# An encoder layer's grid attention: sets of equal length, scores seven steps ahead, and the last input projection ended half by half

## The chip, the cores and the metric

One Trainium2 chip, of which the kernel uses one core. The metric is the device time of one execution in microseconds, lower is better; the time of a kernel is the median of its runs. Engines: PE (TensorE, the matmuls), DVE (VectorE), ACT (ScalarE), POOL (GpSimd) and SP (SyncE, which here only issues DMAs). PEld is the weight load of PE.

## What is computed

One encoder layer on 1024 tokens of width 1024, all in float32:

```
hn   = rmsnorm(h);  proj = hn @ w_in            # 1024 x 2304 columns
o_a  = window attention, 8 heads of 64, 2 kv heads, |i-j| <= 128, a sink logit per head
o_b  = neighbourhood attention, 8 heads of 64, on the 16 x 64 grid of tokens,
       window 8 x 16, with a bias by 2-D offset
h    = h + concat(rmsnorm(o_a), rmsnorm(o_b)) @ w_out
h    = h + (silu(conv3(hn2 @ w_gate)) * (hn2 @ w_up)) @ w_down
out  = rmsnorm(h)
```

## The kernel before

**Precision.** Each float32 operand is held as a high and a low part in the type of the fast matmul. A product of two such operands is three matmuls of 128x512 (`block`, lines 176 to 179): high by high, high by low, low by high. The low part costs a subtraction on DVE, the high part a copy on ACT.

**Stages.** First the input projection: 18 column tiles of 128 (`Project`, m = 0 to 17). Tiles 0 to 5 feed the window heads. From m = 6 on each pair of grid heads has three tiles: the values of both heads, then query and key of the one and of the other, so that head 6 of the grid needs m = 16 and head 7 needs m = 17. Then follow attention, the out projection (`OutA`, the window half, lines 600 to 626; the grid half after it) and the gated MLP, which takes the time from about 365 us to the end.

**How attention and projections are mixed.** PE runs in the order in which the Python code issues (PE alone has a manual schedule). On the other engines the tile framework's scheduler orders the instructions, with priorities. Lines 887 to 914 write PE's order: `flat` holds 16 window units and then 32 grid units, four per grid head. A grid head has eight blocks of 128 queries (`q_step`) and eight blocks of 128 keys (`t_step`), and the four units hold 1, 2, 2 and 3 of the latter (`chunks`, line 556). In each unit there are three kinds of events:

- "q": scores of one query block (line 389, two matmuls into one of two PSUM banks "s"), then its softmax (lines 412 to 420): bias and row minimum on DVE, the exponential on ACT, and for each pair of blocks the scaling on POOL;
- "t", called a set in what follows: two or three transposes of 128x128 (line 526, name pt), whose result is split into ph (ACT, line 426) and pl (DVE, line 427);
- "v": the value products of the set before (lines 537 and 538, which need ph and pl). A set's value products come one set later, behind the next set's transposes.

After each event `fill` draws blocks of three matmuls from `filler`, a generator that runs the rest of the projections and then `OutA`: `RATES` says how many per window of eight units or per grid head, and a unit of a grid head gets a quarter of its head's number, whatever its sets. Scores are drawn with `q_until(u + 2)`: all those of the next two units, at the places 1, 3, 5 and so on of the unit's events. Where scores need a projection that isn't done, `run_q` draws filler blocks until it is; these aren't counted in `debt`.

**From projection to scores.** When a projection's two halves have gone through PSUM (two banks "pj"), `evacuate` scales them on DVE (line 251 for the grid). After some more filler blocks `post` calls `split_qk` (lines 301 to 313): for each half a high part on ACT (line 306) and a low part on DVE (line 307), and then four DMAs on SP's queue that stack parts on the upper and lower partitions: q from a's upper half (line 309), q from b's upper half (310), b's upper half from a's lower one (311), and a's upper half from b's lower one (312). Line 311 overwrites what line 310 reads, and line 312 what line 309 reads. Only then can the head's first scores run.

**The last projection.** m = 17 (lines 582 to 593) runs its two halves in turns, k by k, so that both end together, and between the k steps it makes the high and low parts of the normed window output (`split`, lines 187 to 191: one 128x1024 copy on ACT and one 128x1024 subtraction on DVE, four times), which take over the buffers of the projection's input. Both halves are evacuated at the end; the first `OutA` block takes the bank of the first half.

Of the kernel before, what the change touches and what calls it, by code (L numbers as in the profile page):

```python
# [14 lines left out]
F32R = mybir.dt.float32r  # L15
AF = mybir.ActivationFunctionType
ALU = mybir.AluOpType
# [3 lines left out]
KT = D // 128  # L21
# [12 lines left out]
RATES = [41, 50, 21, 21, 21, 21, 13, 19, 20, 17]  # L34
SPARE = (3, 6)
AHEAD = 2
EVA = (1, 3, 5, 8)
WARM = 8

# [17 lines left out]
def hybrid_layer(tc, xT, w_first, w_in, w_out, w_gate, w_up, w_down, small, sink, rpb, consts, rope, out):  # L57
    nc = tc.nc
    with ExitStack() as ctx:
# [13 lines left out]
        def big(name, tag, dt=F32):  # L73
            return lpool.tile([128, S], dt, name=name, tag=tag, bufs=slots[tag])

        def tmp(name, dt=F32, n=S):
            return tpool.tile([128, n], dt, name=name, tag="t", padded_shape=[128, S + 16])

        def bank(name, tag):
            return psum.tile([128, HALF], F32, name=name, tag=tag)  # L80

        f32 = lambda ap: ap.bitcast(F32)
        tsl = lambda h: slice(h * HALF, (h + 1) * HALF)
# [16 lines left out]
        flat = lambda t, n: t[:, 0:n * 384].rearrange("p (k c) -> p k c", c=384)  # L100
# [3 lines left out]
        for name, dst, n in (("h", his, 2), ("h", his, 2), ("l", los, 2), ("l", los, 2), ("w", None, 2)):  # L104
            t = flat(big(name, "mix", F32R)[:, :], n)
# [46 lines left out]
        def behind(*names):  # L152

            stack = ExitStack()
            for n in names:
                stack.enter_context(tc.issue_after(mark[n].ins))
            return stack
# [18 lines left out]
        def block(ps, w, x, h, first, last):  # L176
            nc.tensor.matmul(ps, w[0], mv(x[0][:, tsl(h)]), start=first, stop=False)  # L177
            nc.tensor.matmul(ps, w[0], mv(x[1][:, tsl(h)]), start=False, stop=False)  # L178
            nc.tensor.matmul(ps, w[1], mv(x[0][:, tsl(h)]), start=False, stop=last)  # L179

        def product(ps, ws, xs, h):

            for i, (w, x) in enumerate(zip(ws, xs, strict=True)):
                block(ps, w, x, h, i == 0, i == len(ws) - 1)
                yield

        def split(src, name, tag):
            hi, lo = big(name + "h", tag, F32R), big(name + "l", tag, F32R)
            nc.scalar.activation(hi, src, AF.Copy)
            nc.vector.tensor_tensor(lo, src, f32(hi[:, :]), op=ALU.subtract)  # L190
            return hi, lo

        def squares(tiles, engine):
            acc = None
# [49 lines left out]
        def evacuate(t, ps, h, grid):  # L244
            if not grid:
                mark["copied"] = nc.vector.tensor_tensor(sv(t[:, tsl(h)]), pv(ps[:, :]), sv(rstd1[:, tsl(h)]), op=ALU.mult)
            else:
                o = t[:, :].rearrange("p (b r s c) -> p r s b c", r=ROWS // 2, s=2, c=8)[:, 4 * h:4 * h + 4]
                i = ps[:, :].rearrange("p (r b c s) -> p r s b c", s=2, b=NB, c=8)
                v = rstd1[:, tsl(h)].rearrange("p (r s b c) -> p r s b c", s=2, b=NB, c=8)  # L250
                nc.vector.tensor_tensor(o, i, v, op=ALU.mult)
# [99 lines left out]
        mix = [None] * 8  # L351
# [14 lines left out]
        def post(m, t):  # L366

            if m < 6:
                turn(m, t)
                stacks(m, t)  # L370
            else:
                hp, i = divmod(m - 6, 3)
                if i == 0:
                    vb[2 * hp], vb[2 * hp + 1] = split_v(t, (0, 1), lambda: done.add(m))
                else:
                    h = 2 * hp + i - 1
                    qb[h], kb[h] = split_qk(t)
# [183 lines left out]
        mg, h1, norm = [None] * 8, [None] * KT, {"halves": 0}  # L561

        class Project:
# [10 lines left out]
            def run(self):  # L574
                self.t = tmp("t")
                if self.m < 17:
                    for h in range(2):
                        ps = bank("pj", "pj")
                        yield from product(ps, self.w, xg, h)
                        with tc.high_priority(offset=500), behind(*["low"] * (self.m == 3 and h == 1)):  # L580
                            evacuate(self.t, ps, h, self.grid)
                else:

                    ps = [bank("pj", "pj") for _ in range(2)]
                    for k in range(KT):
                        for h in range(2):
                            block(ps[h], self.w[k], xg[k], h, k == 0, k == KT - 1)
                            yield
                        if k % 2:
                            mg[k // 2] = split(mix[k // 2], "mg", "xg")  # L590
                    with tc.high_priority(offset=500):
                        for h in range(2):
                            evacuate(self.t, ps[h], h, self.grid)

            def post(self):
                post(self.m, self.t)
                if self.m < 6 or self.m % 3:
                    done.add(self.m)

        class OutA:  # L600
            def __init__(self, d):
# [27 lines left out]
        xg, first = [None] * KT, [Project(m) for m in range(3)]  # L629
# [58 lines left out]
        t = quarters(big("f", "mix"))  # L688
# [136 lines left out]
        def fill(n):  # L825
            while n > 0 and next(filler, False):
                n -= 1
# [3 lines left out]
        for g in range(2):  # L831
            for b in range(NB):
                q, t = unit_window(g, b)
# [7 lines left out]
        flat = []  # L841
        for u, (q, t, need, kind, ahead) in enumerate(units):
            flat.append((q, t, need, kind))
        debt = 0.0
# [6 lines left out]
        order = []  # L851
# [3 lines left out]
        def q_until(u, limit):  # L855
            nonlocal qpos
            res = []
            while qpos < len(queue_q) and queue_q[qpos][0] <= u and len(res) < limit:
                res.append(queue_q[qpos])
                qpos += 1  # L860
            return res

        def run_q(items):
            for u, s in items:
                while any(m not in done for m in flat[u][2]):
                    assert next(filler)
                s()

        sums = {}

        def square_b(u):

            if u == 40:
                sums["b"] = big("sqb", "op")
                for h in range(2):
                    nc.scalar.activation(sums["b"][:, tsl(h)], mix[4][:, tsl(h)], AF.Square)
            s2 = tmp("sq")
            for h in range(2):
                nc.scalar.activation(s2[:, tsl(h)], mix[5 if u == 40 else 6][:, tsl(h)], AF.Square)
                nc.vector.tensor_tensor(sums["b"][:, tsl(h)], sums["b"][:, tsl(h)], s2[:, tsl(h)], op=ALU.add)  # L880

        pend = None
        for i, item in enumerate(q_until(1, 4 + AHEAD)):
            run_q([item])
            fill(i % 2 + 1)
        fill(FILL1 - 9)
        for u in range(len(flat)):
            q, t, need, kind = flat[u]
            if kind == 0 and u < 14:
                mine = q_until(u + 2, 4)  # L890
            else:
                mine = q_until(min(u + 2, len(flat) - 1), 99)
            events = []
            for ts in t:
                events += [("t", ts), ("v", None)]
            for i, item in enumerate(mine):
                events.insert(min(EVA[i] if kind == 0 else 2 * i + 1, len(events)), ("q", item))
            wi = u // 8 if u < 16 else 2 + (u - 16) // 4
            per = RATES[wi] / (8 if u < 16 else 4) / len(events)
            if u in (40, 44):  # L900
                square_b(u)
            for what, e in events:
                if what == "t":
                    nxt = e()
                elif what == "v":
                    if pend is not None:
                        pend()
                    pend = nxt
                else:
                    run_q([e])  # L910
                debt += per
                fill(int(debt))
                debt -= int(debt)
            live["op"] -= 7 if u in (7, 15) else 4 if u >= 16 and u % 4 == 3 else 0
        with tc.high_priority(offset=500), behind("high"):
            nc.scalar.activation(warm, eps, AF.Sqrt)
# [23 lines left out]
        for h in range(2):  # L940
            wide = widen(vb2[h], "pt")
            for i in range(4):
                x = mix[4 + i][:, tsl(h)]
                hi, lo = (t[:, tsl(h)] for t in mg[4 + i])
# [111 lines left out]
        for h in range(2):  # L1056
            for d in range(KT):
                if h == 0 and d + 2 < KT:
                    wo.append(load_wo(d + 2, False))
                ps = bank("pj", ("o", "s", "pj")[(h * KT + d) % 3])  # L1060
# [4 lines left out]
                if h == 1 and d == 1:  # L1065
                    v = inverse_narrow([total[0]], D, "pt")
# [148 lines left out]
        v = inverse_narrow([total[1]], D, "pt")  # L1215
# [50 lines left out]
        order = []  # L1266
# [71 lines left out]
        for i, f in enumerate(FO[HEAD:]):  # L1338
            u = Gated(f)
# [117 lines left out]
        for i, (p, j, c) in enumerate(order):  # L1457
# [10 lines left out]
            ps = banks[p, j]  # L1468
# [8 lines left out]
            q = i % 12  # L1477
# [16 lines left out]
        parts = {}  # L1494
        for k, cols in enumerate(quarters):
            for j in (2, 3):
                ps = banks[6, j]
# [111 lines left out]
```

## Time and profile before

| | us |
|---|---|
| median of 3 runs | 1029.18 (1029.17 to 1029.4) |
| the profiled execution's own time | 1030.14 |
| its span, first to last instruction | 1028.4 |
| PE busy in the span | 1011.9 (98%) |
| DVE, ACT, POOL busy | 836.6, 560.6, 107.7 |

Busy time on PE is rough: matmuls overlap, and a matmul's end is modelled, so that a short stop can hide inside the one before it. Where it matters the distance between the starts of two matmuls is the better measure. The rows of a timeline give start, duration, engine, line, operation, output and inputs; in brackets stands the idle time before the row and what ended it. A queue's name with q at the end (SPq) is the issue of a DMA, not its transfer.

### The profile page before, as it was taken

What the parts mean: (1) busy time and instruction counts of PE and PEld (TensorE: products, weight loads), DVE (VectorE), ACT (ScalarE), POOL (GpSimd) and SP (SyncE); (2) the same over time, 40 slices, a digit from 0 to 9 for tenths busy, and PEclk for the clock granted to TensorE, in tenths of its full rate; (3) what the DMA queues carried; (4) which work ended last, traced back from release to release, by engine and by line L of the source; (5) the groups of instructions that cost most, each with busy time, mean ns of one, the idle gap of its engine ahead of it and who ended that gap; (6) DMA issues with size and microseconds to landing.
All of it is one profiled execution on the core that took longest, in us unless ns stands there. A gap on an engine that the chain in (4) does not pass through costs nothing.

```text
span 1028.4 us, 14846 instructions
## 1 busy us (share of the span) xinstructions
PE 1011.9 (98%) x5094; PEld 889.3 (86%) x5094; DVE 836.6 (81%) x1566; ACT 560.6 (55%) x1077; POOL 107.7 (10%) x188
## 2 busy tenths in 40 slices
PE   9999999999999999999999999999999999999996
PEld 8888888888888888888888888888888888888886
DVE  7889888768888799999987777786787767896765
ACT  8467776657676545565545444443544644554451
POOL 0233332232242100000000000000000000000002
PEclk9999999999999999999999999999999999999998
DMA  7223122333325247313443332233322889866644
GB/s 291 77 77 78 47 72 62 84 81 82 83 61 176 76 164 261 102 50 114 154 185 103 124 121 95 102 113 113 102 111 95 285 281 305 299 237 236 225 149 164
DMA packets 68220, 144.94 MB, mean 141 GB/s; under 512 B 8240, under 2 KB 18736, under 8 KB 68144
## 3 DMA queue, kind: packets, MB, share of 16 engines
q1 hardware_dynamic: 58064, 118.82, 36.0%
q10 hardware_dynamic: 10080, 25.17, 6.3%
q8 instruction: 40, 0.66, 0.3%
q14 instruction: 36, 0.29, 0.1%
HBM read 103.58 MB, written 28.57 MB: 129 GB/s over the span
## 4 chain that ended last, share of the span: by engine, by line
PE 77%; DVE 13%; ACT 4%; DMA 3%; issue 2%; SPq 0%; POOL 0%; DVEq 0%; ACTq 0%; POOLq 0%
PE dn L994 6%; PE dn L992 6%; PE dn L993 6%; PE x L992 6%; PE x L993 6%; PE x L994 6%; PE pj L177 5%; PE pj L178 5%; PE pj L179 5%; PE y L992 3%; PE y L993 3%; PE y L994 3%; PE s L389 3%; PE z L993 2%; PE z L992 2%
## 5 line engine op out<-in xcount | busy, mean ns | idle before, releaser
L992 PE MATMUL x<-hg,whi 128*128 128x512 f32 x352 | 133.7, 380 | 1.2 <-ACT gs L1034 1.2
L993 PE MATMUL x<-hg,whi 128*128 128x512 f32 x352 | 133.4, 379 | 0.0
L994 PE MATMUL x<-hg,wlo 128*128 128x512 f32 x352 | 133.4, 379 | 0.0
L992 PE MATMUL dn<-xd,whi 128*128 128x512 f32 (+1 forms) x330 | 120.8, 366 | 0.0
L993 PE MATMUL dn<-xd,whi 128*128 128x512 f32 (+1 forms) x330 | 120.5, 365 | 0.0
L994 PE MATMUL dn<-xd,wlo 128*128 128x512 f32 (+1 forms) x330 | 120.5, 365 | 0.0
L416 ACT ACTIVATE p<-p,nm 128x385 f32<-128x385 f32 (+3 forms) x128 | 74.9, 586 | 53.8 <-DVE nm L412 50.3
L177 PE MATMUL pj<-xgh,whi 128*128 128x512 f32 x245 | 99.9, 408 | 0.7 <-ACT xgh L637 0.4
L966 ACT ACTIVATE whi<-ws 128x512 fp32r<-128x512 f32 (+1 forms) x100 | 60.7, 621 | 71.9 <-DVE ws L1106 16.5
L420 POOL TENSOR_SCALAR p<-p,sm 128x384 f32<-128x384 f32 (+1 forms) x128 | 78.7, 628 | 198.9 <-DVE sm L418 159.4
L178 PE MATMUL pj<-xgl,whi 128*128 128x512 f32 x245 | 93.0, 379 | 0.3 <-DVE xgl L638 0.3
L179 PE MATMUL pj<-xgh,wlo 128*128 128x512 f32 x245 | 92.9, 379 | 0.0
L966 ACT ACTIVATE whi<-raw 128x512 fp32r<-128x512 f32 (+1 forms) x102 | 60.9, 611 | 44.1 <-PE x L993 20.0
L967 DVE TENSOR_TENSOR wlo<-ws,whi 128x512 fp32r<-128x512 f32 (+1 forms) x100 | 66.6, 679 | 20.1 <-ACT whi L966 19.9
L427 DVE TENSOR_TENSOR pl<-pt,ph 128x384 fp32r<-128x384 f32 (+2 forms) x108 | 63.3, 589 | 20.5 <-ACT ph L426 18.3
L1314 ACT ACTIVATE xd<-xd 128x512 fp32r<-128x512 f32 x77 | 47.5, 626 | 54.5 <-DMA xd<-x 54.0
L992 PEld LDWEIGHTS x<-hg,whi 128*128 128x128 f32 x352 | 66.5, 189 | 11.4 <-ACT gs L1034 2.0
L1315 DVE TENSOR_TENSOR xd<-xd 128x512 fp32r<-128x512 f32 x77 | 52.2, 686 | 29.6 <-ACT xd L1314 29.3
L1429 POOL TENSOR_TENSOR h<-h,wide 128x256 f32<-128x256 f32 (+1 forms) x6 | 5.4, 915 | 672.0 <-ACT wide L1425 672.0
L994 PEld LDWEIGHTS x<-hg,wlo 128*128 128x128 f32 x352 | 66.5, 189 | 9.4
L993 PEld LDWEIGHTS x<-hg,whi 128*128 128x128 f32 x352 | 66.5, 189 | 9.4
L992 PEld LDWEIGHTS dn<-xd,whi 128*128 128x128 f32 x330 | 62.5, 189 | 7.7
(267 smaller groups left out, 2531.7 us busy)
## 6 DMA issues: line engine op xcount, KB each, us to landing
xd<-x SPq DMA_DIRECT2D x77, 256.0 KB, 5.3
raw<-in_w_down_dram SPq DMA_DIRECT2D x72, 256.0 KB, 4.1
raw<-in_w_gate_dram SPq DMA_DIRECT2D x22, 512.0 KB, 3.5
raw<-in_w_up_dram SPq DMA_DIRECT2D x22, 512.0 KB, 3.5
x<-c ACTq DMA_DIRECT2D x22, 512.0 KB, 2.6
raw<-in_w_in_dram SPq DMA_DIRECT2D x30, 256.0 KB, 2.8
raw<-in_w_down_dram SPq DMA_DIRECT2D x36, 192.0 KB, 4.4
x<-t ACTq DMA_DIRECT2D x11, 512.0 KB, 2.6
```

The lines of the kernel that those rows point to most:

```text
L177: nc.tensor.matmul(ps, w[0], mv(x[0][:, tsl(h)]), start=first, stop=False)
L178: nc.tensor.matmul(ps, w[0], mv(x[1][:, tsl(h)]), start=False, stop=False)
L179: nc.tensor.matmul(ps, w[1], mv(x[0][:, tsl(h)]), start=False, stop=last)
L416: nc.scalar.activation(p[:, j, 0:e], p[:, j, 0:e], AF.Exp, bias=nm, scale=-1.0, accum_out=sm[:, j:j + 1])
L420: nc.gpsimd.tensor_scalar(p[:, i, 0:m], p[:, i, 0:m], sm[:, i:i + 1], 1.0, op0=ALU.mult, op1=ALU.mult)
L427: mark["rest"] = nc.vector.tensor_tensor(pl[:, 0:n], ps[:, 0:n], f32(ph[:, 0:n]), op=ALU.subtract)
L966: nc.scalar.activation(hi, src, AF.Copy)
L967: nc.vector.tensor_tensor(lo, src, f32(hi[:, :, :]), op=ALU.subtract)
L992: nc.tensor.matmul(ps, w[0], x[0], start=first and i == 0, stop=False, skip_group_check=True)
L993: nc.tensor.matmul(ps, w[0], x[1], start=False, stop=False, skip_group_check=True)
L994: nc.tensor.matmul(ps, w[1], x[0], start=False, stop=last and i == len(ws) - 1, skip_group_check=True)
L1315: nc.vector.tensor_tensor(lo, f32(lo), f32(hi), op=ALU.subtract)
```

## The change

Four edits, all in the grid attention and in the last projection:

1. The filler of a grid head is spread by sets instead of by units: each set gets an eighth of its head's number (`RATES[...] / 8`), spread evenly over its events.
2. Scores are drawn one per set, and at the first set of the first grid head four at once (`GRID_AHEAD - 3`), so that the scores run seven steps ahead of the sets. Within a set the order is transposes, scores, value products of the set before.
3. Filler blocks that `run_q` draws are taken off `debt`.
4. m = 17 runs k = 0 to 5 in turns as before, then k = 6 and 7 of the first half and k = 6 and 7 of the second; each half is evacuated when it is done. The window output's parts are made 128x512 at a time, the second half one filler block later.

```diff
+GRID_AHEAD = 7
...
-                    for k in range(KT):
-                        for h in range(2):
-                            block(ps[h], self.w[k], xg[k], h, k == 0, k == KT - 1)
-                            yield
-                        if k % 2:
-                            mg[k // 2] = split(mix[k // 2], "mg", "xg")
-                    with tc.high_priority(offset=500):
-                        for h in range(2):
-                            evacuate(self.t, ps[h], h, self.grid)
+                    order = [(k, h) for k in range(KT - 2) for h in range(2)] + [(k, h) for h in range(2) for k in (KT - 2, KT - 1)]
+                    parts = []
+                    for k, h in order:
+                        block(ps[h], self.w[k], xg[k], h, k == 0, k == KT - 1)
+                        if k == KT - 1:
+                            with tc.high_priority(offset=500):
+                                evacuate(self.t, ps[h], h, self.grid)
+                        yield
+                        if parts:
+                            split_part(*parts.pop(0))
+                        if h and k % 2:
+                            i = k // 2
+                            mg[i] = big("mgh", "xg", F32R), big("mgl", "xg", F32R)
+                            split_part(i, 0)
+                            parts.append((i, 1))
+                    for part in parts:
+                        split_part(*part)
...
+        def split_part(i, h):
+            src, (hi, lo) = mix[i][:, tsl(h)], (t[:, tsl(h)] for t in mg[i])
+            nc.scalar.activation(hi, src, AF.Copy)
+            nc.vector.tensor_tensor(lo, src, f32(hi), op=ALU.subtract)
...
                 while any(m not in done for m in flat[u][2]):
                     assert next(filler)
+                    debt -= 1
                 s()
...
-            if kind == 0 and u < 14:
-                mine = q_until(u + 2, 4)
+            events = []
+            if kind == 0:
+                mine = q_until(u + 2, 4 if u < 14 else 99)
+                for ts in t:
+                    events += [("t", ts), ("v", None)]
+                for i, item in enumerate(mine):
+                    events.insert(min(EVA[i], len(events)), ("q", item))
+                rate = [RATES[u // 8] / 8 / len(events)] * len(events)
             else:
-                mine = q_until(min(u + 2, len(flat) - 1), 99)
-            events = []
-            for ts in t:
-                events += [("t", ts), ("v", None)]
-            for i, item in enumerate(mine):
-                events.insert(min(EVA[i] if kind == 0 else 2 * i + 1, len(events)), ("q", item))
-            wi = u // 8 if u < 16 else 2 + (u - 16) // 4
-            per = RATES[wi] / (8 if u < 16 else 4) / len(events)
+                rate = []
+                for ts in t:
+                    mine = q_until(len(flat) - 1, 1 if events or u > 16 else GRID_AHEAD - 3)
+                    events += [("t", ts)] + [("q", item) for item in mine] + [("v", None)]
+                    rate += [RATES[2 + (u - 16) // 4] / 8 / (2 + len(mine))] * (2 + len(mine))
...
-                fill(int(debt))
-                debt -= int(debt)
+                due = max(0, int(debt))
+                fill(due)
+                debt -= due
```

More of the change, by code (lines that the diff above doesn't have):

```diff
@@ L185, in product @@
                 yield
[L187 to L191, printed above, removed]
         def squares(tiles, engine):
@@ L863, in run_q @@
         def run_q(items):
+            nonlocal debt
             for u, s in items:
@@ L888, in hybrid_layer @@
             q, t, need, kind = flat[u]
-            if kind == 0 and u < 14:
-                mine = q_until(u + 2, 4)
-            else:
-                mine = q_until(min(u + 2, len(flat) - 1), 99)
-            events = []
-            for ts in t:
-                events += [("t", ts), ("v", None)]
-            for i, item in enumerate(mine):
-                events.insert(min(EVA[i] if kind == 0 else 2 * i + 1, len(events)), ("q", item))
-            wi = u // 8 if u < 16 else 2 + (u - 16) // 4
-            per = RATES[wi] / (8 if u < 16 else 4) / len(events)
+            events = []
[6 more added lines that the diff above has]
+                rate = [RATES[u // 8] / 8 / len(events)] * len(events)
+            else:
+                rate = []
[3 more added lines that the diff above has]
+                    rate += [RATES[2 + (u - 16) // 4] / 8 / (2 + len(mine))] * (2 + len(mine))
             if u in (40, 44):
                 square_b(u)
-            for what, e in events:
+            for (what, e), per in zip(events, rate, strict=True):
                 if what == "t":
```

## The prediction

> **What bounds the kernel now.** I read the page first, then the busy time of PE in the stretch that the change touches, then who PE waits for there, then the timeline around those waits.
>
> ```profile
> span 1028.4 us, 14846 instructions
> PE 1011.9 (98%) x5094; PEld 889.3 (86%) x5094; DVE 836.6 (81%) x1566; ACT 560.6 (55%) x1077; POOL 107.7 (10%) x188
> ```
> ```profile
> 186.00:345.00 159.00, 155.11 (x890) 136.87 (x890) 128.92 (x312) 105.92 (x255) 48.58 (x70) 1.00 0.35 98
> ```
> ```profile
> PE o L538 <- DVE pl L427: 2.0, 5, 1.0
> PE pj L177 <- DVE t L251: 0.7, 1, 0.7
> PE pj L177 <- DVE v L339: 0.3, 1, 0.3
> PE o L537 <- ACT ph L426: 0.3, 1, 0.3
> PE s L389 <- DMA kb<-ka: 0.2, 1, 0.2
> ```
>
> PE is the bound: 98% busy. The change reorders PE and adds no matmul (the built programs have the same PE instructions), so it can only make or remove stops of PE. In the grid attention, 186 to 345 us, PE is busy for 155.11 of 159.00 us, so 3.9 us show as idle, 3.5 of them in nine waits. Idle time hides inside the matmul before it:
>
> ```profile
> 205.28 0.33 PE L537 MATMUL o<-ph,v 128*128 128x384 f32 x1
> 205.44 0.33 PE L538 MATMUL o<-pl,v 128*128 128x384 f32 x1
> 206.04 0.38 PE L178 MATMUL pj<-xgl,whi 128*128 128x512 f32 x1
> 206.26 0.38 PE L179 MATMUL pj<-xgh,wlo 128*128 128x512 f32 x1
> 206.50 0.43 PE L537 MATMUL o<-ph,v 128*128 128x384 f32 x1
> 207.09 0.43 PE L538 MATMUL o<-pl,v 128*128 128x384 f32 x1 [0.16 <-DVE pl L427]
> ```
>
> Undisturbed, L538 starts 0.16 us after L537 (205.44). At 207.09 it starts 0.59 after, a stop of 0.43 us where the row shows 0.16. With 0.27 hidden in each of some 12 stops (the nine listed and a few too short to be listed) the stretch loses 3.9 + 12 x 0.27 = 7.1 us. That is what the change can win.
>
> **What the change removes.** These are the stops before the value products. A set's value products wait for pl; between a set's transposes and its value products stood two filler blocks for the seventh set of nearly every head (a unit with three sets got no more filler than one with a single set), mostly four elsewhere. In the changed order it is three to six, two only twice, in head 4. A block is three matmuls at 0.216 us (206.04 to 206.26), 0.65 us, so the seventh set gains 0.65 to 1.9 us where it was short by 0.43. I count these stops as gone (2.3 us listed with L537's). The wait of 0.7 us for L251 is this one:
>
> ```profile
> 311.55 0.49 PE L526 MATMUL pt<-cst,p 128*128 128x128 f32 x3
> 312.75 0.45 PE L177 MATMUL pj<-mgh,whi 128*128 128x512 f32 x1 [0.71 <-DVE t L251]
> ```
>
> The first `OutA` block needs the bank of m = 17's first half. Now that half ends 2.5 us of PE ahead of `OutA` instead of 1.6, and its evacuation doesn't stand behind the other half's end: 0.95 us gone with the hidden part (312.75 less the 0.25 us that three transposes take from 311.55). The wait behind v goes too, as no new bank is opened right after those transposes. Splitting the parts moves no DVE time worth counting:
>
> ```profile
> L190 DVE TENSOR_TENSOR mgl<-mixa,mgh 128x1024 fp32r<-128x1024 f32 x4 | 6.0, 1514 | 0.2 <-ACT mgh L189 0.2
> L170 DVE TENSOR_TENSOR wlo<-raw,whi 128x512 fp32r<-128x512 f32 x17 | 13.3, 783 | 1.7 <-ACT whi L169 1.7
> ```
>
> Four of 1.51 us become eight of 0.68 to 0.78; DVE is the cover, and it is off the path unless a pl stands behind it. **Gain: 7.0 us; bounds 4.0 (the listed waits alone, half of the hidden part) and 7.5.**
>
> **What the change adds.** Scores seven steps ahead means that head h+1's first scores come some three sets earlier, while the projections come when they came. For heads 1 to 5 the projection is ready 15 us or more before; heads 6 and 7 need m = 16 and m = 17, the last two. Before, their chains end just in time. Head 6:
>
> ```profile
> 294.55 0.38 PE L179 MATMUL pj<-xgh,wlo 128*128 128x512 f32 x1
> 304.37 0.27 PE L389 MATMUL s<-ka,q 128*128 128x256 f32 x1
> ```
> ```profile
> 295.07 0.68 DVE L251 TENSOR_TENSOR t<-pj,rstd 128x512 f32<-128x512 f32 x1
> 296.54 1.41 DVE L307 SCALAR_TENSOR_TENSOR kb<-t,cst,ka 128x512 fp32r<-128x512 f32 x2
> ```
> ```profile
> 297.98 0.47 SPq L310 DMA_DIRECT2D q<-kb  x1
> 301.29 0.46 SPq L311 DMA_DIRECT2D kb<-ka  x1
> ```
>
> m = 16's last matmul starts at 294.55; the scores run at 304.37, 9.6 us after its end at 294.76. And head 7:
>
> ```profile
> 318.95 1.41 DVE L307 SCALAR_TENSOR_TENSOR kb<-t,cst,ka 128x512 fp32r<-128x512 f32 x2
> ```
> ```profile
> 320.38 0.47 SPq L310 DMA_DIRECT2D q<-kb  x1
> 323.46 0.46 SPq L311 DMA_DIRECT2D kb<-ka  x1
> ```
> ```profile
> 326.05 0.27 PE L389 MATMUL s<-ka,q 128*128 128x256 f32 x1
> 326.48 0.38 PE L389 MATMUL s<-kb,q 128*128 128x256 f32 x1 [0.16 <-DMA kb<-ka]
> ```
>
> The second low part ends at 320.36; L310 is issued at once, L311 waits 3.1 us for it to land, lands in turn, and the scores go on at 326.48: **6.1 us from the end of L307 to the scores**, and PE waits already. (In head 6 the two issues are 3.3 apart.)
>
> In the changed order the end of m = 16 and the first scores of head 6 are separated by five filler blocks, two score products, one pair of value products and three transposes, 4.0 us of PE instead of 9.6; from m = 17 to head 7's scores it is 5.8. The scheduler's order on DVE and ACT makes it tighter still. For head 6 the second L307 stands behind a pl whose transposes end only three blocks, 1.95 us, before the scores; for head 7 it stands behind the first `OutA` half's addition (L623) and one softmax step, and that half's last matmul ends two blocks, a pair of value products and three transposes, 1.85 us, before the scores. From those points:
>
> ```profile
> L426 ACT ACTIVATE ph<-pt 128x384 fp32r<-128x384 f32 x43 | 20.7, 482 | 9.2 <-PE pt L526 8.9
> L427 DVE TENSOR_TENSOR pl<-pt,ph 128x384 fp32r<-128x384 f32 x43 | 23.8, 553 | 9.5 <-ACT ph L426 9.2
> L623 DVE TENSOR_TENSOR h<-pj,xr 128x512 f32<-128x512 f32 x7 | 4.8, 679 | 0.0
> L412 DVE CUSTOM_DVE_ANT_1 p<-s,xb 128x256 f32<-128x256 f32 x15 | 6.2, 414 | 0.3 <-PE s L389 0.3
> L307 DVE SCALAR_TENSOR_TENSOR kb<-t,cst,ka 128x512 fp32r<-128x512 f32 x12 | 9.2, 777 | 0.0
> ```
>
> Head 6: 0.3 from PE's end to the next engine (294.76 to 295.07), 0.48 + 0.55 + 0.78 + 6.1 = 8.2, less the 2.06 to the second score matmul: PE stops for 6.1 us at least. Ahead of that pl ACT has an exponential and a head's output copy and DVE the sum of that output, so up to 1 us more. Head 7: 0.3 + 0.68 + 0.41 + 0.08 + 0.78 + 6.1 = 8.35, less 1.96: 6.4 us. All of PE stands behind these scores, in order; nothing covers it. **I take 6.5 each, 13.0; bounds 5.5 (both DMAs a little faster) and 7.7 each.**
>
> **The clock.** A PE that stands still loses its clock, as the end of the kernel shows:
>
> ```profile
> 1018.59 0.28 PE L994 MATMUL dn<-xd,wlo 128*128 128x256 f32 x1
> ```
> ```profile
> 1020.00:1021.00 1.00, 0.43 (x4) 0.35 (x4) 0.17 (x1) 0.26 (x1) 0.00 (x0) 1.00 0.75 261
> 1021.00:1021.50 0.50, 0.42 (x3) 0.46 (x4) 0.00 (x0) 0.00 (x0) 0.00 (x0) 0.75 0.44 150
> 1021.50:1022.00 0.50, 0.50 (x3) 0.10 (x1) 0.38 (x1) 0.00 (x0) 0.00 (x0) 0.50 0.00 0
> ```
> ```profile
> 0.99 3.51 PE L146 MATMUL warm_ps<-ones 128*128 128x128 f32 x16 [0.99 <-POOL eps L141]
> ```
>
> The last dense matmul starts at 1018.59, and between 1021.0 and 1021.5, some 2.5 us of little work later, the granted clock falls to half (0.75 is half of that stretch). A stop of 6.5 us is longer. Coming back takes about 3 us, an estimate from the 16 matmuls at the start, the first of the kernel: 0.22 us each, 3.51 in all, where three transposes of that size at 311.55 take 0.49 with the last one's tail. At half clock 3 us do the work of 1.5. **Two stops: 3.0 us more; bounds 0 and 5.0.** [...]
>
> **Small new waits.** The first set of head 0 issues two pairs of scores close together; with two PSUM banks the fourth waits for a softmax step of 0.55 us in DVE's queue. With a few short stops like it 0.8 us; bounds 0 and 1.5. The stop of head 7's scores in before (0.2 listed) is in the 7.0 and replaced by the new one.
>
> **Sum.** +13.0 + 3.0 + 0.8 - 7.0 = +9.8 us. The profiled execution took 1030.14 us (span 1028.4 and 1.7 around it), so the changed one comes to 1039.9; the median is 1.0 lower, 1029.18, and gives **1039.0 us**.
>
> **The rivals.**
>
> *Full clock.* The stops come, but PE keeps its clock or regains it at once. For: within the stretch the clock never fell. Against: no stop there exceeds 1.3 us. 1029.18 + 6.8 = 1036.0.
>
> *The gain fails.* The seventh set's wait is DVE's queue (129 of 159 us busy), not too little filler, and reappears elsewhere; then the gain is some 3 us, and the rest stays: 1043.0. Against: in before the seventh set is where it stops, head after head, and it has the least filler.
>
> *Faster.* The mechanism is the chain from projection to scores in heads 6 and 7: if both parts are stacked before PE gets there, no stop arises. That needs 2.0 us from the last releaser where the rows give 8.2; it decides at that point alone. Then 1029.18 + 0.8 - 7.0 = 1023.0. I see nothing in the rows for it, unless DVE and ACT get to the parts earlier than their order allows.
>
> **How the numbers follow.** Forecast 1036.5 to 1042, 62%; full clock 16%; the gain fails 12%; faster 6%; the rest, 4%, mostly longer stops. The low end takes both stops at 5.5, no clock loss, the gain of 7.5: +3.5, 1033; the high end 7.7 each, 3.0 for the clock, a gain of 4.0: +14.4, 1043.5. Within 0.2%, about what a measurement can tell from no change, 2%; slower 92%; faster 6%.
>
> **What would show it.** Two stops of PE at the score line (L389 before) behind the DMA kb<-ka, some 4 and 6 us of PE after the ends of m = 16 and m = 17, 6 to 7 us each; granted clock 0.5 for some 3 us behind each; the waits on pl nearly gone; no wait for L251 before the first `OutA` block; PE's busy time longer by the half-clock matmuls. Wrong it is if the waits on kb are under 4 us, or if the value products still wait.

## The result and the profile after

| | before | after |
|---|---|---|
| median, us | 1029.18 | 1044.17 (1043.43 to 1045.19) |
| ratio | | 1.0144, 95% interval 1.0132 to 1.0156 |
| the profiled execution | 1030.14 | 1043.92 |
| its span | 1028.4 | 1042.1 |

The change made the kernel 1.44% slower, 15.0 us by the medians and 13.7 by the spans. The forecast was 1039.0 with a range of 1033.0 to 1043.5: the sign and the mechanism came true, and the time lies just above the range.

Line numbers shifted: in the kernel after, the scores are L384 (L389 before), the low parts of q and k L302 (L307), the stacking DMAs q<-kb L305 (L310), kb<-ka L306 (L311) and ka<-kb L307 (L312), the evacuation L246 (L251), pl L422 (L427), transposes L521 (L526), value products L532 and L533 (L537 and L538), and a block's matmuls L178 to L180 (L177 to L179).

The page's head of the kernel after:

```profile
span 1042.1 us, 14870 instructions
...
PE 1015.3 (97%) x5094; PEld 894.5 (86%) x5094; DVE 836.2 (80%) x1570; ACT 564.1 (54%) x1081; POOL 113.9 (11%) x188
```

There are as many PE instructions as before (5094), but 3.4 us more busy time: matmuls at a lower clock (0.51 of full in 305.00:311.00 below). These are the same stretch as was read of before, and four pieces of it (columns: stretch, length, busy time of PE, PEld, DVE, ACT and POOL, granted clock, DMA share, GB/s):

```profile
186.00:345.00 159.00, 143.49 (x805) 127.62 (x804) 117.88 (x293) 101.23 (x243) 51.48 (x66) 0.96 0.32 87
304.00:305.00 1.00, 0.12 (x1) 0.15 (x1) 0.00 (x0) 0.00 (x0) 0.00 (x0) 0.52 1.03 229
305.00:311.00 6.00, 5.30 (x17) 4.62 (x18) 2.52 (x7) 2.76 (x7) 0.00 (x0) 0.51 0.07 15
331.00:338.20 7.20, 5.07 (x15) 4.29 (x16) 1.29 (x4) 1.61 (x4) 0.00 (x0) 0.53 0.55 182
338.20:345.00 6.80, 6.80 (x40) 6.20 (x40) 5.43 (x14) 4.04 (x10) 1.04 (x2) 1.00 0.37 116
```

PE is idle for 15.5 of 159 us instead of 3.9, and twice the clock falls to half, from about 304.0 to 310.9 and from about 331.4 to 338.2 us. What PE waits for (total, times, longest):

```profile
PE s L384 <- DMA ka<-kb: 10.5, 2, 5.6
PE s L384 <- DMA kb<-ka: 2.0, 2, 1.3
PE pt L521 <- DVE pl L422: 1.5, 1, 1.5
...
PE pj L178 <- DVE t L246: 0.7, 1, 0.7
...
PE vt L329 <- DVE pl L422: 0.4, 1, 0.4
```

The waits of the value products on pl (2.0 us in five in before) are gone, though 1.9 us of waits on pl stand at other places (the rows with pt and vt), and the scores wait for the stacking DMAs: 12.5 us in four waits. PE's rows around both stops, and two rows from each stretch of half clock:

```profile
298.88 0.38 PE L180 MATMUL pj<-xgh,wlo 128*128 128x512 f32 x1
304.88 0.55 PE L384 MATMUL s<-ka,q 128*128 128x256 f32 x1 [5.62 <-DMA ka<-kb]
306.13 0.55 PE L384 MATMUL s<-kb,q 128*128 128x256 f32 x1 [0.69 <-DMA kb<-ka]
...
308.18 0.63 PE L178 MATMUL pj<-xgh,whi 128*128 128x512 f32 x1
308.61 0.63 PE L179 MATMUL pj<-xgl,whi 128*128 128x512 f32 x1
...
326.63 0.38 PE L180 MATMUL pj<-mgh,wlo 128*128 128x512 f32 x1
331.85 0.55 PE L384 MATMUL s<-ka,q 128*128 128x256 f32 x1 [4.84 <-DMA ka<-kb]
333.68 0.55 PE L384 MATMUL s<-kb,q 128*128 128x256 f32 x1 [1.28 <-DMA kb<-ka]
```

By the distance of starts, less the 0.22 us of the block's last matmul and the 0.11 of a score product, head 6 loses 6.00 - 0.22 + 1.25 - 0.11 = 6.9 us and head 7 loses 5.22 - 0.22 + 1.83 - 0.11 = 6.7. In the half-clock stretch a 128x512 matmul takes 0.43 us instead of 0.22. The chain that PE waits for, on DVE and in SP's queue:

```profile
299.18 0.73 DVE L302 SCALAR_TENSOR_TENSOR kb<-t,cst,ka 128x512 fp32r<-128x512 f32 x1
```
```profile
299.95 0.47 SPq L305 DMA_DIRECT2D q<-kb  x1
...
303.18 0.46 SPq L306 DMA_DIRECT2D kb<-ka  x1
```
```profile
326.75 0.74 DVE L302 SCALAR_TENSOR_TENSOR kb<-t,cst,ka 128x512 fp32r<-128x512 f32 x1
```
```profile
327.52 0.47 SPq L305 DMA_DIRECT2D q<-kb  x1
...
330.60 0.46 SPq L306 DMA_DIRECT2D kb<-ka  x1
```

From the end of L302 to the second score product it is 306.13 - 299.91 = 6.2 us in head 6 and 333.68 - 327.49 = 6.2 in head 7, and the DMA that overwrites waits 3.1 to 3.2 us for the one that reads.

In head 6 the scores even overtook the projection in PE's order: three filler blocks stand in a row ahead of its first score (they start at 297.07, 297.80 and 298.45; the last ends with the row at 298.88), and two of them are drawn by `run_q`, because m = 16 isn't done when its scores are due. By the order that the code writes this happens nowhere else in after, and nowhere in before, rate_only, rates23 or a run with a shorter lead, so edit 3 moves two blocks in after and nothing in those.

### The profile page after: what moved, and what is told of

It is laid out like the page before. It is cut to its first block, busy times and chain, and to the rows that moved or that the text cites. A ratio compares the mean times of both kernels' runs of the same rounds, so it can differ in the third digit from the quotient of the medians.

```text
span 1042.1 us, 14870 instructions
## 1 busy us (share of the span) xinstructions
PE 1015.3 (97%) x5094; PEld 894.5 (86%) x5094; DVE 836.2 (80%) x1570; ACT 564.1 (54%) x1081; POOL 113.9 (11%) x188
## 4 chain that ended last, share of the span: by engine, by line
PE 78%; DVE 13%; DMA 3%; ACT 3%; issue 2%; POOL 0%; SPq 0%; DVEq 0%; ACTq 0%; POOLq 0%
PE dn L1008 6%; PE dn L1006 6%; PE dn L1007 6%; PE x L1006 6%; PE x L1007 6%; PE x L1008 6%; PE pj L178 5%; PE pj L179 5%; PE pj L180 5%; PE s L384 3%; PE y L1008 3%; PE y L1007 3%; PE y L1006 3%; PE pt L447 2%; PE z L1008 1%
## 5 line engine op out<-in xcount | busy, mean ns | idle before, releaser
L415 POOL TENSOR_SCALAR p<-p,sm 128x384 f32<-128x384 f32 (+1 forms) x128 | 83.3, 663 | 197.0 <-DVE sm L413 156.1
L178 PE MATMUL pj<-xgh,whi 128*128 128x512 f32 x245 | 100.1, 409 | 0.9 <-DVE t L246 0.7
L179 PE MATMUL pj<-xgl,whi 128*128 128x512 f32 x245 | 93.3, 381 | 0.0
L180 PE MATMUL pj<-xgh,wlo 128*128 128x512 f32 x245 | 93.1, 380 | 0.0
L422 DVE TENSOR_TENSOR pl<-pt,ph 128x384 fp32r<-128x384 f32 (+2 forms) x108 | 63.5, 589 | 24.9 <-ACT ph L421 23.0
```

The costliest lines, as they stand in the source:

```text
L415: nc.gpsimd.tensor_scalar(p[:, i, 0:m], p[:, i, 0:m], sm[:, i:i + 1], 1.0, op0=ALU.mult, op1=ALU.mult)
L422: mark["rest"] = nc.vector.tensor_tensor(pl[:, 0:n], ps[:, 0:n], f32(ph[:, 0:n]), op=ALU.subtract)
```

## The experiments

The theory after the trace: PE stops because the scores of heads 6 and 7 are placed closer to the end of their projection than the chain is long; each stop takes the clock with it. Rivals: the chain is held up in DVE's or SP's queue whatever PE's order is, or the last projection's new form is in its way. A second question is where the other 4.5 us of new stops come from. In each set of runs, before came to 1029.0 to 1029.3 us.

### How far ahead the scores run

```
-GRID_AHEAD = 7
+GRID_AHEAD = 6    (lead6; 5: lead5; 4: lead4)
```

> The changed kernel with scores six steps ahead instead of seven. By the chain theory a first score of head 6 or 7 needs about 9.0 and 8.7 us from the last PE event that its parts wait for (the changed kernel: 2.06 and 1.96 us of PE in between, stops of 6.9 and 6.7). Here the order gives 1.85 and 3.9 us, so stops of 7.1 and 4.8, the clock still halved after both: 1042.5 us. If the stops come from the last projection's new form and not from the lead, both stay at 6.8 and the time at 1044.

> Five steps ahead. Chain theory: 4.0 and 6.8 us of PE in between, so stops of 5.0 and 1.8 us, the clock halved after the first only (2.2 us back): 1035 us. The rival, that the lead isn't it: 1044.

> Four steps ahead. Chain theory: 6.95 and 9.1 us in between, so stops of 2.0 and 0, full clock, and the burst of scores at head 0 gone too: 1027.3 us, below the kernel before. The rival, that the lead isn't it: 1043. If equal sets win nothing: 1031 to 1033.

Measured: lead6 1037.28 us (ratio 1.008, 1.0064 to 1.0095), lead5 1030.49 (1.0015, 1.0006 to 1.0025), lead4 1026.16 (0.9974, 0.9963 to 0.9985). Each step less of lead takes time off, and with four steps the rest of the change is a gain. What is left of the two stops in lead4 is one wait of head 6:

```profile
302.42 0.27 PE L384 MATMUL s<-ka,q 128*128 128x256 f32 x1
303.50 0.38 PE L384 MATMUL s<-kb,q 128*128 128x256 f32 x1 [0.80 <-DMA kb<-ka]
```

The expectations for lead6 and lead5 were some 5 us too high. In lead6 both stops are shorter than in after (6.2 and 4.3 us), and of the small stops some 2.4 us are left of 4.5. In lead5 the stops are 3.9 and 1.9 us and the profiled execution, the shortest of ten, kept its full clock; the executions group by their granted clock: 0.997 in the one of 1028.46 us, 0.996 in five of 1029.35 to 1030.53, 0.995 in four of 1031.24 to 1032.02. The means of these groups are 1.6 and 1.7 us apart. That fits a stop of 3.9 us that halves the clock in some executions and not in others, but only the one that kept it has a trace.

### Filler earlier, scores as far ahead as in the change

Theory and rival differ most if the scores stay seven steps ahead and only the projections come sooner.

```
-RATES = [41, 50, 21, 21, 21, 21, 13, 19, 20, 17]
+RATES = [41, 50, 23, 23, 23, 23, 13, 16, 17, 15]    (rates23)
+RATES = [41, 50, 23, 23, 23, 22, 12, 17, 18, 15], GRID_AHEAD = 5    (lead5_rates23)
```

> Kernel after with one line changed, RATES = [41, 50, 23, 23, 23, 23, 13, 16, 17, 15]: two more projection steps a set in heads 0 to 3, fewer in heads 5 to 7, the scores still seven steps ahead. By the order of the instructions TensorE then has 9.4 and 10.7 us of work between the last releaser of the chain and the first scores of heads 6 and 7, where after has 2.0 and 1.9. Theory (the chain of about 6.1 us is given too little work to stand beside): both stops and both stretches at half clock go, 13.6 + 4.5 us, and 1044.2 - 18.1 = 1026.1 us is left; with the other small stops moved, 1024 to 1029. Rival (the chain waits in DVE's and SP's queues, so that it slips along however early the filler is issued): stops of over 3 us stay, 1036 or more.

> Kernel after with the scores five steps ahead and RATES = [41, 50, 23, 23, 23, 22, 12, 17, 18, 15]: by the order of the instructions 14.5 and 12.7 us of TensorE work beside the chains of heads 6 and 7. Theory: no stop there, and the stops that the run with four steps had (5.9 us in the stretch from 180 to 345 us, 1.0 of it before head 6) are not more: 1024 to 1026.2 us. Rival (more filler ahead crowds DVE in heads 0 to 3, where the scores' evacuations then come late): as slow as before or slower, 1029 or more.

Measured: rates23 1022.74 us (ratio 0.994, 0.9925 to 0.9955), lead5_rates23 1022.56 (0.9941, 0.9926 to 0.9956). Both beat both kernels, and both lie some 1.3 us below the range that was expected of them; the 0.2 us between them can't be told apart. The same stretch of rates23 and the first scores of heads 6 and 7:

```profile
186.00:345.00 159.00, 157.76 (x923) 141.78 (x923) 128.09 (x323) 110.63 (x266) 49.21 (x72) 1.00 0.35 98
```
```profile
299.23 0.36 PE L384 MATMUL s<-ka,q 128*128 128x256 f32 x1
299.80 0.38 PE L384 MATMUL s<-kb,q 128*128 128x256 f32 x1 [0.22 <-DMA kb<-ka]
...
317.53 0.36 PE L384 MATMUL s<-ka,q 128*128 128x256 f32 x1
317.72 0.28 PE L384 MATMUL s<-kb,q 128*128 128x256 f32 x1
```

PE idles for 1.2 of 159 us and the clock stays full. One line of numbers turns a loss of 15.0 us into a gain of 6.5. The rival is right in one small part. In head 6 of rates23 the chain itself is 2.0 us longer: L302 ends at 291.63 and the second score starts at 299.80, 8.2 us later instead of 6.2, because L307 (ka<-kb) is issued only at 295.60, after a wait of 3.4 us for the DMA q<-ka. The 9.4 us of work beside it still leave a stop of only 0.5 us. So the chain can be held up in SP's queue, but the stops of after come from too little work beside it. Over all runs, the PE work in program order between the last PE instruction that the chain waits for and the head's first score, and the stop measured there:

| | work beside head 6, 7 | stop, head 6, 7 | sum |
|---|---|---|---|
| before | 8.5, 8.5 | 0, 0.4 | -, 8.9 |
| after | 2.0, 1.9 | 6.9, 6.7 | 8.9, 8.6 |
| lead6 | 1.9, 3.9 | 6.2, 4.3 | 8.1, 8.2 |
| lead5 | 4.0, 6.8 | 3.9, 1.9 | 7.9, 8.7 |
| lead4 | 7.0, 9.1 | 1.0, 0 | 8.0, - |
| rate_only (below) | 6.0, 6.6 | 3.0, 1.9 | 9.0, 8.5 |
| rates23 | 9.4, 10.7 | 0.5, 0 | 9.9, - |

The work is that of 0.216 us a 128x512 matmul and so on. Stop and work make 7.9 to 9.0 us together in every row but head 6 of rates23, whose longer chain was just shown; that is the chain's length from PE to PE. Below that, each microsecond of work taken away is, within 1 us, a microsecond of stop.

### What the clock costs

Matmuls of a constant tile into the score bank, ahead of the first score of heads 6 and 7, keep PE busy during the stop and change nothing else of the work.

```
+            for _ in range(idle):
+                nc.tensor.matmul(ps[:, 0:128], ones, ones, start=True, stop=True)
...
-                    ps, n = scores(qb[h], kb[h], b)
+                    ps, n = scores(qb[h], kb[h], b, 54 if b == 0 and h > 5 else 0)    (warm54; 29: warm29)
```

> The changed kernel with 54 matmuls of 128x128 on a constant (0.11 us each at full clock, 6.0 us) ahead of the first scores of head 6 and of head 7, written into the bank that these scores then overwrite: PE works where it stood still. If the slow matmuls behind the stops are the clock's, they go: 1044.2 - 4.5 = 1039.7 us and granted clock 1.0 there. If they are not (waits of another kind), the time stays at 1044 or grows by what the added matmuls exceed the stop.

> Kernel after with 29 matmuls of the constant tile of ones into the score bank ahead of the first score of heads 6 and 7 (29 and not 54: in the run with 54 one of them took 0.22 us, its 108 passes lying from 298.8 to 310.8 us, so that they were longer than the stop). 29 x 0.222 = 6.4 us fills a stop of 6.9 or 6.7 us almost and lengthens nothing. Theory (the clock that falls in the stop costs 2.3 us behind each of the two, beside the stop): the clock stays full and the time is 1044.2 - 4.5 = 1039.7 us. Rival 1 (the price that was forecast, 1.5 us each): 1041.2. Rival 2 (the half clock lies beside other waits and costs nothing): 1044.2.

warm54 came to 1049.36 us (ratio 1.0194, 1.0179 to 1.021) and missed, because these matmuls took twice what was assumed. The group of head 6 alone:

```profile
L383 PE MATMUL s<-ones x108: 273/275/275, 298.9 to 310.8; 128*128 128x128 f32 x108
```

Each is recorded as two matmuls of 0.11 us, so that 54 take 12.0 us, longer than the stop. They outlast the stops of 6.9 and 6.7 by 10.4 us together; less the clock's 4.6, found next, that makes 5.8 us more than after, where 5.2 were measured. With 29, warm29 came to 1039.56 (ratio 1.0102, 1.0085 to 1.0119): full clock (0.997 over the execution, as in before; 0.991 in after), and hardly a wait for the DMAs:

```profile
PE s L386 <- DMA kb<-ka: 0.6, 2, 0.3
```

The second score product of head 6 starts at 305.90 (in after at 306.13), so PE gets on no earlier, and **the clock's share is 1044.17 - 1039.56 = 4.6 us**, shown by itself. The rows give it too: at half clock, from the second score at 306.13 to 310.9 and from 333.68 to 338.2, PE works for 4.8 and 4.5 us and loses half of that, 2.4 and 2.3.

### The two other halves of the change alone

rate_only is before with edit 1 alone; last_only is before with edit 4 alone, last_old is after with edit 4 undone.

```
-            per = RATES[wi] / (8 if u < 16 else 4) / len(events)
+            per = RATES[wi] / 8 * (1 if u < 16 else len(t)) / len(events)    (rate_only)
```

> Kernel before with the filler alone changed to sets of equal length (as much behind each event of a head, whether its set has one score step or three); the scores and the last projection as before. By the order of the instructions the chains of heads 6 and 7 then have 6.0 and 6.6 us of TensorE work beside them, and over the runs so far that work and the stop made 8 to 9 us together, so stops of 2.4 and 1.8 us are expected there, where before has 0.1 and 0.4. Theory A (the stops ahead of the value products of the seventh sets came of little filler beside them, which is what the gain of 7 us was put on): these go and 1029.2 - 7.0 + 3.7 = 1025.9 us is left, 1024 to 1027.5. Rival (they go only where the scores run further ahead): they stay, and 1029.2 + 3.7 = 1032.9.

> Kernel before with the last projection alone changed (its first half ends ahead of the second, low parts split by halves of 512). Theory: the wait of 0.95 us for the evacuation of the last projection goes and nothing comes: 1029.2 - 0.95 = 1028.2 us. Rival 1 (the splits, now twice as many instructions on DVE and ScalarE, come in the way of heads 6 and 7): 1029.2 or more.

> Kernel after with the last projection as in before. Theory (the last projection is in neither of the two stops, which lie ahead of it or wait for another chain): 1044.2 us, and at most 0.95 more for the evacuation that was waited for in before. Rival (its splits by halves stand in DVE's and ScalarE's queues ahead of the chain of head 7): the stop at 327 us is shorter by 1 us or more, 1043 or less.

rate_only came to 1031.3 us (ratio 1.0025, 1.0016 to 1.0034), between its two expectations. The seventh sets' stops went in every head, so more filler beside them covers them. But the stops at heads 6 and 7 are 3.0 and 1.9 us, the first costs clock as well, and around 260 and 280 us others of 4.0 us arise, which no theory had; their cause in this kernel wasn't tried. Edit 2 was not run alone. Head 6's stop, and the clock in it and behind it:

```profile
303.45 0.35 PE L389 MATMUL s<-ka,q 128*128 128x256 f32 x1 [1.80 <-DMA ka<-kb]
304.60 0.54 PE L389 MATMUL s<-kb,q 128*128 128x256 f32 x1 [0.80 <-DMA kb<-ka]
```
```profile
301.00:304.60 3.60, 1.00 (x7) 0.53 (x5) 2.65 (x5) 3.41 (x7) 3.60 (x5) 1.00 0.74 162
304.60:308.10 3.50, 3.50 (x9) 2.99 (x10) 2.39 (x4) 1.55 (x3) 1.42 (x1) 0.51 0.00 0
```

last_only came to 1029.07 us (ratio 0.9999, 0.9989 to 1.0008): the gain of 0.95 did not come. The wait for the evacuation (L251) did go, and the next value product, which before waited 0.49 us for pl, waits 0.92. The row of before, and two of last_only:

```profile
315.48 0.43 PE L538 MATMUL o<-pl,v 128*128 128x384 f32 x1 [0.49 <-DVE pl L427]
```
```profile
313.23 0.43 PE L537 MATMUL o<-ph,v 128*128 128x384 f32 x1
314.58 0.43 PE L538 MATMUL o<-pl,v 128*128 128x384 f32 x1 [0.92 <-DVE pl L427]
```

last_old came to 1044.54 us, within the scatter of after, and its two stops, by the same count, are 6.9 us each: edit 4 causes neither.

### The small stops near the fourth head

The two largest small stops of after stand where DVE has eight multiplies that normalise the first half of the mix. Two runs placed these differently in the code:

```
-            aux[13, 1 + i + i // 2] = normed_a(*divmod(i, 2))
+            aux[13 + i // 4, 1 + 4 * (i % 4)] = normed_a(*divmod(i, 2))    (norm_before, norm_after)
```

> Kernel before with the eight normalising multiplies of the first half of the mix (0.74 us each on DVE, all within one projection, from 268 to 281 us) put at every fourth step of two projections. Theory (the largest stop of before, 1.6 us at 273.6 to 275.6 us, is DVE's queue at that place and not little filler): it goes, 1029.2 - 1.6 = 1027.6 us. Rival (it comes of little filler, as the other seventh sets): it stays, 1029.2.

> Kernel after with the same multiplies spread over two projections in the same way. Theory (the new stops of after at 279 and 281 us, 2.25 us in all, are the same pile-up on DVE, met at another place of the order): 1044.2 - 2.2 = 1042.0 us. Rival (they come of the scores, or the split of the values, at that place): 1044.2.

They told nothing: the scheduler put the multiplies where they had been, and the order of every engine is that of before and of after. As repeats they gave 1029.45 and 1043.87 us. So the multiplies were left out:

```
-        for i in range(8):
-            aux[13, 1 + i + i // 2] = normed_a(*divmod(i, 2))    (skip_after, skip_before)
```

> Kernel after without the eight normalising multiplies of the first half of the mix (that part of the normalisation is left out; 8 x 0.74 us on DVE between 270 and 284 us). Theory (the new stops of after at 279 and 281 us, 0.6 + 1.6 us, are DVE's queue, which holds these multiplies ahead of the evacuations that TensorE waits for): both go, 1044.2 - 2.2 = 1042.0 us. Rival (the low parts of the values and the scores' own evacuations fill DVE there by themselves): at least 1.5 us of the two stays, 1043.5 or more.

> Kernel before without the same eight multiplies. Theory (the largest stop of before, 1.6 us at 273.6 to 275.6 us ahead of a seventh set's value product, is the same queue on DVE): it shrinks to the 0.5 us of the other early heads, 1029.2 - 1.1 = 1028.1 us. Rival (little filler beside that set, as in the other heads): it stays, 1029.2.

Measured: skip_after 1041.28 us, 2.9 less than after (expected 1042.0); skip_before 1028.07, 0.9 less than before in the same set (expected 1028.1; ratio 0.9991, 0.9981 to 1.0001, so the time alone doesn't tell, and the rows do). The rows of the place in before and in skip_before:

```profile
274.07 0.43 PE L537 MATMUL o<-ph,v 128*128 128x384 f32 x1
275.50 0.43 PE L538 MATMUL o<-pl,v 128*128 128x384 f32 x1 [1.00 <-DVE pl L427]
```
```profile
273.15 0.33 PE L537 MATMUL o<-ph,v 128*128 128x384 f32 x1
273.42 0.43 PE L538 MATMUL o<-pl,v 128*128 128x384 f32 x1
```
The first distance falls from 1.43 to 0.27 us. And after, its DVE and then its PE, with skip_after's PE last:

```profile
277.28 2.14 DVE L824 SCALAR_TENSOR_TENSOR mixa<-mixa,par,rstda 128x512 f32<-128x512 f32 x2
279.35 0.55 DVE L422 TENSOR_TENSOR pl<-pt,ph 128x384 fp32r<-128x384 f32 x1
```
```profile
281.26 0.33 PE L533 MATMUL o<-pl,v 128*128 128x384 f32 x1
283.06 0.52 PE L521 MATMUL pt<-cst,p 128*128 128x128 f32 x3 [1.48 <-DVE pl L422]
```
```profile
280.33 0.33 PE L533 MATMUL o<-pl,v 128*128 128x384 f32 x1
280.71 0.52 PE L521 MATMUL pt<-cst,p 128*128 128x128 f32 x3
```

In after the transposes start 1.80 us behind the value product, in skip_after 0.38. So before's largest stop and after's largest small one have the same cause, DVE's queue behind these multiplies, met at two places of PE's order.

## Why the prediction was right or wrong

- **PE is the bound, and the change can only make or remove its stops.** Right: the terms below add up to the difference between the medians within 0.3 us.
- **Two stops of 6.5 us, 13.0.** Right, 6.9 and 6.7, 13.6: behind the DMA kb<-ka's chain, with 6.2 us from L302 (L307 before) to the scores where 6.1 was read off. The rates23 and lead runs show that the distance to the projection is the cause.
- **Half clock, 3.0 us.** Right in kind, too small: 4.6, within the bounds of 0 to 5.0. What was mis-sized is "coming back takes about 3 us", the author's estimate from the matmuls at the kernel's start, where the trace of before gives a granted clock of 1.00 from 0.99 to 4.50 us. No run shows the 3 us: in after the half clock lasted 6.8 us each time, each stop was in two parts, and PE worked for 4.8 and 4.5 us at half clock behind the second. The rows at the kernel's end are no measure of a stop either: the clock fell there some 2.5 us after the last dense matmul, with PE still busy in part (0.43 of the 1.00 us from 1020.00).
- **Small new waits, 0.8 us.** This is the step that failed: the term is 4.5 us, three times its own bound of 1.5. The burst of scores at 186 us is there as described, 0.8 us. Not foreseen were 0.5 at 262 us, 0.6 and 1.6 at 279 and 281, and 0.9 at 295, where an evacuation stands behind a pl. The two at 280 are DVE's multiplies, shown by skip_after; those at 262 and 295 are read from the waits alone and weren't tried. The working looked for new stops where scores are issued, and not for places where a changed order of PE meets DVE's queue.
- **Gain, 7.0 us.** Right in size: the stops of before in the stretch, those of 0.1 us and more by the distance of starts, come to 7.4 us, and nearly all left their place. But "a seventh set lacks filler" was not the whole cause in the fourth head, whose stop of 1.6 us stood behind DVE's queue and came back as 2.2 a few microseconds later. And the 0.95 of the evacuation is no gain by itself: in last_only it came back as a wait for pl.
- **Sum.** 13.6 + 4.6 + 4.5 - 7.4 = 15.3 us, against 15.0 between the medians and +9.8 forecast. Of the 5.5 us too little, 3.7 are the small waits, 1.6 the clock and 0.6 the stops, less 0.4 of a larger gain. In the two profiled executions the grid attention, from its first transposes (184.08 before, 184.01 after) to its last value products (355.48 and 370.25), is 14.8 us longer; the spans differ by only 13.7, because all that follows took 1.1 us more in that execution of before, which was 1.0 us above its median.
- **The range.** Its high end, 1043.5, was added from two stops of 7.7, 3.0 for the clock and a gain of 4.0. It left out the small waits and took the clock's middle value, although their own bounds were 1.5 and 5.0; with these it would have been 1047.1, above the 1044.17 measured.
- **The rivals.** Full clock is refuted by the rows and by warm29. Faster did not happen, but its condition, enough work beside the chain, is what rates23 supplies, and its 1023.0 is near the 1022.74 of that run, in part by luck: some 2 us of small stops are left there, where 0.8 was put in. "The gain fails" was half true: the waits behind DVE reappeared, the ones for lack of filler did not.

## What to carry to other kernels

Where an engine runs in a written order, measure each chain that leaves it and comes back (here 8 to 9 us from the last PE instruction that it waits for to the scores) and count the work that the order puts beside it: moving the consumer forward without moving the producer cost microsecond for microsecond here (within 1 us in the table), and 4.6 us of clock on top. Of each wait that an edit is to remove, ask whether the releaser was late for lack of cover or for its own queue; here the first kind went away when work was spread, and the second came back at another place. When a reordering loses, look for the knob that moves the other end of the chain before undoing it.

## What the runs showed of the hardware

How long PE stood still before the granted clock fell was not one length: 4.9 us in head 6 of after (no matmul from 299.1, half clock from about 304.0), but about 2.4 us in head 7 of lead6 (PE waited there 2.4 us for ka<-kb, 7.3 in the two heads less the longer of 4.9, and the clock was at half from 327.6 on, row 327.60:334.40). Nor need a single gap be long: in rate_only two waits of 1.80 and 0.80 us by the rows, with one score product between them, halved the clock (0.51 in 304.60:308.10), where lead5's waits of 2.67 and 0.83 us did not in the profiled execution (1.00 in 186.00:345.00). Why the one did and the other did not, no trace tells. The clock was then at half for 6.8 us at both stops of after (304.0 to 310.9, 331.4 to 338.2) and, in lead6, over the 6.7 us from 300.30 and the 6.8 from 327.60, although PE ran again long before the end, and for 3.4 us in rate_only, whose stop of 3.0 us ended as the clock fell (row 304.60:308.10). What sets these lengths was not shown. The second stop of lead6 and what came behind it:

```profile
327.60:334.40 6.80, 5.54 (x15) 4.48 (x16) 1.64 (x4) 1.09 (x4) 0.00 (x0) 0.50 0.90 297
334.40:345.00 10.60, 10.60 (x63) 9.64 (x62) 7.53 (x19) 5.47 (x15) 2.19 (x4) 1.00 0.23 75
```

In warm54 a plain float32 matmul of 128x128 took 0.22 us and was recorded as two of 0.11 (54 of them are the 108 rows from 298.9 to 310.8; granted clock 0.997 over the execution). At the start of before eight of them, 16 rows in 3.51 us, took 0.44 each, at a granted clock of 1.00.
